# A hybrid attention encoder layer on one core: three placements in the schedule and the output norm's inverse root on GpSimd

## The chip, the cores and the metric

The kernel runs on one core of a Trainium2 chip. The metric is the device time of one execution in microseconds (us). The core has TensorE (PE, matrix products; its weight loads are listed as PEld), VectorE (DVE), ScalarE (ACT), GpSimd (POOL) and SyncE (SP, which issues nearly all the transfers here). Each engine executes its own instructions strictly in order and waits on semaphores for the others. A tile in PSUM, the memory that matrix products are written to, can be written again only when its last reader is done.

## The reference

Input x is 2048 x 1024, float32. One projection gives the columns of two mixers: gated linear attention (GLA: four heads, forward and backward scans, summed) and latent attention (MLA: four heads, low-rank query and key/value, softmax over all 2048 positions). Their gated outputs, 512 columns each, go through one output projection, and a layer norm over the scaled residual gives the result:

```python
def reference(x, ...):
    mixed = hybrid_mixer(x, ...)
    return layer_norm(DEEPNORM_ALPHA * x + mixed, ln_g, ln_b)

def hybrid_mixer(x, positions, w_in, ...):
    h = x @ w_in
    ... = jnp.split(h, idx, axis=-1)
    o_a = gla_branch(...)      # o = rms_norm(o_fwd + o_bwd, norm_g); return o * silu(gate)
    o_b = mla_branch(...)      # s = q_nope k_nope + q_rope k_rope; softmax(s) v; return o * silu(gate)
    return jnp.concatenate([o_a, o_b], axis=-1) @ w_out

def layer_norm(t, g, b):
    mu = jnp.mean(t32, axis=-1, keepdims=True)
    var = jnp.mean(jnp.square(t32 - mu), axis=-1, keepdims=True)
    return (t32 - mu) * lax.rsqrt(var + LN_EPS) * g + b
```

## The kernel before

The 2048 positions are cut into 16 chunks of 128. Every float32 product that needs the accuracy is made of three fast passes: each operand is split into a high part (`hi`, L378, on ACT, by rounding) and a low part (`lo`, L384, on DVE or POOL), and `mm3` (L432 to L434) adds high x high, low x high and high x low in PSUM.

The program has four stages. Sweeps A and B (to about 347 us) make the projections and scans of the linear attention. **Sweep C** (about 347 to 572 us) walks over the chunks two at a time, in 8 steps (st). For each chunk it projects the latent inputs (`ipm`, L1363), normalises and transposes them (`cq`, `ckv`, `tm`), finishes the linear attention's output, and for each step makes the gate of the second mixer. The pieces that matter here are these.

- The GLA output of a chunk: `Ob` is a matrix product in PSUM; `oib` (L1531, DVE) adds the part inside the chunk; `sqO` (L1535, ACT) squares; `ss` (L1540, L1541, DVE) sums; `rgl` and `rgd` make the inverse root; `og` (L1551, DVE) multiplies and so reads `Ob` for the last time; `oT` (L1557) transposes.
- The gate of a step: `pz` is a PSUM tile with a half for each of the two chunks, j = 0 and 1; `gm1`, `gm2`, `gm3` (L1287, L1291, L1295, ACT) make its sigmoid; `gm4` (L1299, DVE) multiplies; `gmx` (L1303, DVE) transposes into `gm`, which SP stores (L1309, `gm_s`).
- The queries of a step: `pqr` and its rope, and `pq`, a PSUM tile. `Ob`, `pz` and `pq` share one PSUM pool (`gp`), so that a new tile of one waits for the last reader of an older one of another.

The order of the instructions in sweep C is given by tables of due places, in units of a step: a task stands where its number says, for instance `gm1=(0.855, 1.309)` for the chunks j = 0 and 1 of a step. `PLACE_C` holds for the middle steps, `PLACE_C_FIRST` for the first step, `PLACE_C_LAST` for the last. The places move an instruction in the queue of its own engine; no data dependence changes.

**Attention** (about 572 to 1100 us) is a loop over 16 blocks i of 512 queries of one head, with 8 tiles j of 256 keys each. `scores` (L1633 to L1637) writes ten matmuls into a PSUM tile of two halves e, of which there are two in all; `copy` (L1642, ACT) takes it out; `smax` (L1652, L1655, DVE) keeps a running maximum in `rm`. At the end of a block `tmax` (L1661, PE) transposes `rm`, `rmax` (L1666, DVE) reduces it to `mc`, and `bmax` (L1673, PE) spreads it to the PSUM tile `mb`. Then `sub` (L1679, DVE), `exp` (L1683, ACT) and the product with the values follow, interleaved with the scores of the next block. Here too a list of places sets the order: `put(t, ...)` puts a call at place t = 8 i + j.

The **output projection** (about 1100 to 1252 us) works chunk by chunk on 16 chunks: the gate (`of`, L1999) and the low parts (`ol`) on POOL, `oh` on ACT, 48 matmuls, then on DVE the residual (L2066; L2057 for the last chunk), the statistics `bn`, their mean and variance `mv` (L2075), `u` = variance + epsilon (L2076), two passes that subtract the mean and scale (L2078), the inverse root of u, and two passes that multiply by it and add the shift (L2081). Each of these two is followed by a store (L2082, SP). The inverse root is `rsqrt`: a logarithm and an exponential on ACT (L445, L446), and a Newton step as three instructions on DVE (L452 to L454).

Of the kernel before, what the change touches and what calls it, by code (L numbers as in the profile page):

```python
# [9 lines left out]
F32 = mybir.dt.float32  # L10
# [3 lines left out]
ALU = mybir.AluOpType  # L14
# [4 lines left out]
P = 128  # L19
# [10 lines left out]
QB = 512  # L30
# [107 lines left out]
    tq=(1.44, 1.56),  # L138
# [4 lines left out]
    kvx=(1.06, 1.48),  # L143
# [15 lines left out]
    kvx=(1.3, 1.44),  # L159
# [7 lines left out]
    tq=(1.13, 1.56),  # L167
    xh=(-0.19, -0.054),
    sqO=(0.272, 0.94),
    rgl=(0.283, 1.029),  # L170
# [10 lines left out]
    oT=(0.392, 1.103),  # L181
    oib=(0.24, 0.881),
    ss=(0.278, 1.005),
    rgd=(0.359, 1.067),
    og=(0.391, 1.102),
    ssm=(0.277, 0.958),
    rmd=(0.401, 1.006),
# [20 lines left out]
    gm1=(0.45, 0.823),  # L208
    gm2=(0.46, 0.826),
    gm3=(0.47, 0.829),  # L210
    gm4=(0.745, 0.832),
    gmx=(0.76, 0.835),
# [20 lines left out]
)  # L233
PLACE_C_FIRST = dict(
    skv=1.6,
    kvx=(1.18, 1.5),
    ipa=(-1.874, 0.381),
    ipb=(-1.582, 0.655),
    ipc=(-0.643, 0.818),
# [1 line left out]
    Ob=(0.066, 0.896),  # L241
    tm=(0.445, 1.143),
    pqr=(0.716, 1.336),
    tq=(1.18, 1.53),
    xh=(-0.3, 1.403),
    sqO=(0.469, 0.999),
    rgl=(0.603, 1.027),
    sqm=(0.073, 0.865),
    rml=(0.101, 0.976),
    cq=(0.33, 1.098),  # L250
# [4 lines left out]
    ckvTh=(0.483, 1.183),  # L255
    krT=(0.871, 1.252),
    qrTh=(1.276, 1.598),
    oT=(0.805, 1.172),
    oib=(0.459, 0.956),
    ss=(0.596, 1.015),  # L260
    rgd=(0.636, 1.064),
    og=(0.804, 1.171),
    ssm=(0.095, 0.913),
    rmd=(0.194, 1.009),
    krf=(-0.407, 0.869),
    cqTl=(0.579, 1.316),
    ckvTl=(0.54, 1.33),
# [17 lines left out]
    gm1=(0.623, 0.643),  # L285
    gm2=(0.6231, 0.815),
    gm3=(0.6232, 0.82),
    gm4=(0.65, 0.83),
    gmx=(0.81, 0.835),
    sgm=1.056,  # L290
    pq=1.431,
    qah=1.57,
# [12 lines left out]
    tq=(0.95, 2.1),  # L305
    xh=(-0.262, -0.109),
    sqO=(0.15, 0.4265),
    rgl=(0.229, 0.429),
# [10 lines left out]
    oT=(0.4285, 0.432),  # L319
    oib=(0.063, 0.426),  # L320
    ss=(0.188, 0.428),
    rgd=(0.25, 0.43),
    og=(0.26, 0.431),
    ssm=(0.1025, 0.53),
    rmd=(0.427, 0.605),
# [17 lines left out]
    lx=(-0.48, -0.573),  # L343
    soT=(1.29, 2.304),
    pz=(0.572, 0.578, 0.707, 0.845, 0.918, 1.023, 1.1, 1.22),
    gm1=(0.855, 1.309),
    gm2=(0.91, 1.608),
    gm3=(1.2, 1.859),
    gm4=(1.26, 1.953),
    gmx=(1.265, 1.954),  # L350
    sgm=2.042,
    pq=1.525,
    qah=1.948,
# [13 lines left out]
class K:  # L367
    def __init__(self, tc, ins, out):
        self.tc, self.nc, self.ins, self.out = tc, tc.nc, ins, out
        self.ulate = []  # L370
        self.qt = {}
        self.parts = {}
# [1236 lines left out]
    def attention(self):  # L1609
        tc, nc = self.tc, self.nc  # L1610
        mm = nc.tensor.matmul
        V, G, Ac = nc.vector, nc.gpsimd, nc.scalar
        NP = NKT // 2
        with ExitStack() as ctx:
# [5 lines left out]
            pM, pO, pX, pA, pS = bank("pM"), bank("pO"), bank("pX"), bank("pA"), bank("pS", 2)  # L1620
# [1 line left out]
            nb = len(blocks)  # L1622
            stt = [dict(s=[None] * NP) for _ in blocks]

            def scores(i, j):


                d = stt[i]
                qh, ql, rh, rl = self.qt[i]
                ps = d["ps", j] = pS.tile([P, 2, QB], F32, tag="pS", name=f"pS{i}_{j}")  # L1630
                for e in range(2):
                    kh, kl, kr = (t[:, 2 * j + e] for t in (self.ckvT_h, self.ckvT_l, self.kr))
                    mm(ps[:, e], kh, qh, start=True, stop=False)  # L1633
                    mm(ps[:, e], kh, ql, start=False, stop=False)  # L1634
                    mm(ps[:, e], kl, qh, start=False, stop=False)  # L1635
                    mm(ps[:, e], kr, rh, start=False, stop=False)  # L1636
                    mm(ps[:, e], kr, rl, start=False, stop=True)  # L1637
# [183 lines left out]
            def put(place, fn, *a):  # L1821
                todo.append((place, len(todo), fn, a))

            def at(f, i, j=None):
                p = PLACE_LAST.get(f, PLACE[f]) if i == nb - 1 else PLACE[f]
                return p[j] if isinstance(p, tuple) else p
# [6 lines left out]
            for i in range(nb):  # L1833
                for j in range(NP):
                    t = NP * i + j
                    put(t, scores, i, j)
                    for n, f in (("copy", copy), ("max", smax), ("sub", sub), ("exp", exp), ("hi", phi), ("lo", plo),
                                 ("pv", pv), ("acc", acc)):
                        if n != "acc" or j != SUM_POOL[0] or i == nb - 1:
                            put(t + at(n, i, j), f, i, j)  # L1840
                put(NP * i + at("acc0", i), acc0, i)
                for n, f in (("tmax", tmax), ("rmax", rmax), ("bmax", bmax)) + {nb - 1: (), nb - 2: own_late}.get(i, own):
                    put(NP * i + NP - 1 + at(n, i), f, i)
                if i + 2 < nb:
                    put(NP * i + 4.05, self.fetch, i + 2)
# [93 lines left out]
class OutProj:  # L1939
# [3 lines left out]
    def __init__(self, kern, ctx, qp, bp, sp, ps, pa, pb, pc, pd):  # L1943
        self.k, self.nc, self.qp, self.bp, self.sp, self.ps = kern, kern.nc, qp, bp, sp, ps
        self.single = (pa, "mb"), (pb, "x"), (pc, "o"), (pd, "ap")
        self.sm = ctx.enter_context(kern.tc.tile_pool(name="smo", bufs=2, reuse_waits="tile"))
        self.raw, self.W, self.gr = {}, {}, {}

    def slot(self, name, dt=F32):
# [119 lines left out]
    def finish(self, o):  # L2069
        kern, nc, sm = self.k, self.nc, self.sm  # L2070
        V, Ac = nc.vector, nc.scalar
        c, rr = o["c"], o["rr"]
        mv = sm.tile([P, 2], F32, tag="mv", name=f"mv{c}")
        u = sm.tile([P, 1], F32, tag="u", name=f"u{c}")
        V.bn_aggr(mv, o["bn"])  # L2075
        V.tensor_scalar(u, mv[:, 1:2], LN_EPS, None, ALU.add)  # L2076
        for n in range(2):
            V.scalar_tensor_tensor(rr[:, n], rr[:, n], mv[:, 0:1], self.ln[0][:, n], ALU.subtract, ALU.mult)  # L2078
        rs = kern.rsqrt(sm, u, 1, f"ln{c}")
        for n in range(2):  # L2080
            V.scalar_tensor_tensor(rr[:, n], rr[:, n], rs, self.ln[1][:, n], ALU.mult, ALU.add)  # L2081
            nc.sync.dma_start(kern.out[c * P:(c + 1) * P, n * 512:(n + 1) * 512], rr[:, n])  # L2082
# [70 lines left out]
```

## Time and profile before

| what | us |
|---|---|
| median of three runs | 1254.19 (1253.59 to 1255.71) |
| the profiled execution | 1253.2 |
| its span, first to last instruction | 1251.4 |
| TensorE busy | 1231.4 |
| VectorE busy | 910.5 |
| ScalarE busy | 732.5 |
| GpSimd busy | 727.8 |

The granted TensorE clock was 0.998 of full speed. In a timeline a row gives the start, the duration, the engine, the line, the operation with its output and inputs, the shapes, and in brackets how long the engine had stood idle before it and what ended the wait. Buffer numbers are left out of the names, and neighbouring instructions of one kind are drawn together (x2, x3). In a list of waits the three numbers are the total, the times and the longest.

### The profile page before, as it was taken

To read this page: it belongs to the slowest core of one execution; us is meant where nothing else is said; L and a number is where in the kernel's file an instruction comes from. 1 tells how busy PE (TensorE), PEld (TensorE's weight loads), DVE (VectorE), ACT (ScalarE), POOL (GpSimd) and SP (SyncE) were. 2 spreads that over 40 slices of the span, in tenths; PEclk is the share of its full clock that TensorE was granted. 3 is DMA by queue.
4 is the path that set the end of the run, shared out by engine and by line. 5 is a ranking of instruction groups with operands and counts; after the bars stand their busy time and mean duration, and the time that the engine had idled before them with its cause. 6 is when DMAs were issued, how large, how long until landed. Compare 5 with 4: busy or idle time off the path is not lost.

```text
span 1251.4 us, 18903 instructions
## 1 busy us (share of the span) xinstructions
PE 1231.4 (98%) x6464; PEld 1066.7 (85%) x6464; DVE 910.5 (73%) x1698; ACT 732.5 (59%) x1173; POOL 727.8 (58%) x443
## 2 busy tenths in 40 slices
PE   8999999999999999999999999999999999999997
PEld 7999999999888889888788888888888888888886
DVE  6635454544566777675999999999999998388776
ACT  7543434344565555545888888888888888411110
POOL 0132323232345555521798888889999999954650
PEclk9999999999999999999999999999999999999999
DMA  8224555555757888859543333313356310376652
GB/s 297 76 80 128 136 143 139 142 136 147 260 178 210 247 253 245 256 177 209 92 69 65 60 59 62 75 24 76 76 112 123 79 43 25 126 241 220 202 189 82
DMA packets 311568, 173.95 MB, mean 139 GB/s; under 512 B 212806, under 2 KB 264910, under 8 KB 311472
## 3 DMA queue, kind: packets, MB, share of 16 engines
q1 hardware_dynamic: 310352, 170.62, 51.0%
q0 software_dynamic: 672, 2.10, 0.4%
q8 instruction: 51, 0.84, 0.3%
q14 instruction: 45, 0.37, 0.1%
q10 hardware_dynamic: 448, 0.03, 0.0%
HBM read 113.93 MB, written 67.14 MB: 145 GB/s over the span
## 4 chain that ended last, share of the span: by engine, by line
PE 90%; DVE 3%; ACT 2%; issue 2%; DMA 2%; POOL 1%; SPq 0%; DVEq 0%; POOLq 0%; ACTq 0%
PE ipm L1363 5%; PE o L432 5%; PE o L434 5%; PE o L433 5%; PE pS L1633 5%; PE pS L1635 5%; PE pS L1634 5%; PE pS L1637 5%; PE pS L1636 5%; PE ipa L432 4%; PE ipa L434 4%; PE ipa L433 4%; PE po L433 3%; PE po L434 3%; PE po L432 3%; PE ipg L434 2%
## 5 line engine op out<-in xcount | busy, mean ns | idle before, releaser
L384 POOL TENSOR_TENSOR pl<-s,ph 128x1024 fp32r<-128x1024 f32 x128 | 306.7, 2414 | 47.2 <-ACT ph L378 37.0
L1642 ACT ACTIVATE s<-pS 128x1024 f32<-128x1024 f32 x128 | 131.4, 1027 | 52.1 <-PE pS L1637 47.1
L1655 DVE TENSOR_TENSOR rm<-pS,rm 128x512 f32<-128x512 f32 x210 | 144.8, 689 | 18.2 <-ACT s L1642 12.7
L1679 DVE TENSOR_TENSOR s<-s,mb 128x1024 f32<-128x1024 f32 x128 | 151.2, 1213 | 8.9 <-PE mb L1673 8.8
L378 ACT ACTIVATE ph<-s 128x1024 fp32r<-128x1024 f32 x128 | 134.8, 1056 | 15.6 <-PE o L434 15.0
L1683 ACT ACTIVATE s<-s 128x1024 f32<-128x1024 f32 x128 | 131.5, 1051 | 10.5 <-DVE s L1679 9.6
L432 PE MATMUL ipa<-wah,xah 128*128 128x384 f32 (+1 forms) x384 | 128.5, 335 | 5.0 <-ACT wah L378 5.0
L433 PE MATMUL ipa<-wal,xah 128*128 128x384 f32 (+1 forms) x384 | 124.3, 324 | 0.6 <-DVE wal L384 0.5
L434 PE MATMUL ipa<-wah,xal 128*128 128x384 f32 (+1 forms) x384 | 124.1, 323 | 0.0
L1105 POOL TENSOR_TENSOR Sb<-Sb,Us 64x512 f32<-64x512 f32 x15 | 19.9, 1325 | 169.9 <-DVE Us L1097 160.8
L1633 PE MATMUL pS<-qh,kvT 128*128 128x512 f32 x256 | 102.6, 401 | 0.8 <-DVE rm L1655 0.4
L432 PE MATMUL o<-ph,vh 128*128 128x512 f32 x256 | 101.0, 395 | 0.0
L1635 PE MATMUL pS<-qh,kvT 128*128 128x512 f32 x256 | 100.0, 391 | 0.0
L1634 PE MATMUL pS<-ql,kvT 128*128 128x512 f32 x256 | 99.9, 390 | 0.0
L1637 PE MATMUL pS<-rl,kvT 128*128 128x512 f32 x256 | 99.8, 390 | 0.0
L1636 PE MATMUL pS<-rh,kvT 128*128 128x512 f32 x256 | 99.7, 390 | 0.0
L434 PE MATMUL o<-ph,vl 128*128 128x512 f32 x256 | 99.7, 390 | 0.0
L433 PE MATMUL o<-pl,vh 128*128 128x512 f32 x256 | 99.6, 389 | 0.0
L1706 DVE TENSOR_TENSOR ap<-ap,s 128x512 f32<-128x512 f32 x120 | 82.9, 691 | 2.6 <-ACT s L1683 0.7
L432 PEld LDWEIGHTS ipa<-wah,xah 128*128 128x128 f32 x384 | 72.6, 189 | 8.4 <-ACT wah L378 5.6
L433 PEld LDWEIGHTS ipa<-wal,xah 128*128 128x128 f32 x384 | 72.7, 189 | 1.9 <-DVE wal L384 1.4
L384 POOL TENSOR_TENSOR ol<-of,oh 128x512 fp32r<-128x512 f32 x32 | 42.6, 1332 | 52.5 <-ACT oh L378 47.1
(309 smaller groups left out, 3286.3 us busy)
## 6 DMA issues: line engine op xcount, KB each, us to landing
xcf<-xT_dram SPq DMA_DIRECT2D x16, 512.0 KB, 5.4
xr<-x_dram SPq DMA_DIRECT2D x16, 512.0 KB, 6.4
out_dram<-rr SPq DMA_DIRECT2D x32, 256.0 KB, 3.8
xaf<-xT_dram SPq DMA_DIRECT2D x14, 512.0 KB, 4.2
oib<-oi_s SPq DMA_DIRECT2D x16, 256.0 KB, 4.8
qdb<-qd_s SPq DMA_DIRECT2D x16, 256.0 KB, 3.5
SU<-su_s SPq DMA_DIRECT2D x16, 256.0 KB, 5.0
ub<-u_s SPq DMA_DIRECT2D x16, 256.0 KB, 4.2
```

The source lines that it names most:

```text
L378: return nc.scalar.activation(dst, src, AF.Copy).ins
L384: return e.tensor_tensor(dst, src, hi.bitcast(F32), ALU.subtract).ins
L432: mm(out, ah, bh, start=start, stop=False)
L433: mm(out, ah, bl, start=False, stop=False)
L434: mm(out, al, bh, start=False, stop=stop)
L1633: mm(ps[:, e], kh, qh, start=True, stop=False)
L1634: mm(ps[:, e], kh, ql, start=False, stop=False)
L1635: mm(ps[:, e], kl, qh, start=False, stop=False)
L1636: mm(ps[:, e], kr, rh, start=False, stop=False)
L1637: mm(ps[:, e], kr, rl, start=False, stop=True)
L1655: V.tensor_tensor(d["rm"], src[:, e], d["rm"], ALU.max)
L1679: V.tensor_tensor(s, s, d["mb"][:, None, :].to_broadcast([P, 2, QB]), ALU.subtract)
```

## The change

Four things change.

1. In `PLACE_C_FIRST`, the first step of sweep C, the last part of chunk 1's linear-attention output moves ahead of the second gate's transposes and of the key/value transposes (`kvx`, `tq`).
2. In `PLACE_C_LAST`, the last step, the sigmoid of the first gate (`gm1` to `gmx`, j = 0) moves from 0.855 behind 1.25, past work of the next chunk.
3. In attention the scores of the second block's second tile are put as two halves, the first 0.6 of a place earlier, so that it stands ahead of `bmax` of the first block.
4. In the output norm the inverse root of u becomes one instruction on POOL, u to the power of −0.5, issued ahead of the two passes that subtract the mean. Logarithm, exponential and Newton step go away.

```diff
 PLACE_C_FIRST = dict(
-    kvx=(1.18, 1.5),
+    kvx=(1.245, 1.5),
...
-    tq=(1.18, 1.53),
+    tq=(1.246, 1.53),
...
-    sqO=(0.469, 0.999),
-    rgl=(0.603, 1.027),
+    sqO=(0.469, 0.941),
+    rgl=(0.603, 0.977),
...
-    oT=(0.805, 1.172),
-    oib=(0.459, 0.956),
-    ss=(0.596, 1.015),
-    rgd=(0.636, 1.064),
-    og=(0.804, 1.171),
+    oT=(0.805, 0.979),
+    oib=(0.459, 0.94),
+    ss=(0.596, 0.9455),
+    rgd=(0.636, 0.978),
+    og=(0.804, 0.9785),
...
-    rmd=(0.194, 1.009),
+    rmd=(0.194, 0.9775),
...
-    gm4=(0.65, 0.83),
-    gmx=(0.81, 0.835),
+    gm4=(0.65, 0.943),
+    gmx=(0.942, 0.9457),
...
 PLACE_C_LAST = dict(
-    gm1=(0.855, 1.309),
-    gm2=(0.91, 1.608),
-    gm3=(1.2, 1.859),
-    gm4=(1.26, 1.953),
-    gmx=(1.265, 1.954),
+    gm1=(1.25, 1.309),
+    gm2=(1.26, 1.608),
+    gm3=(1.27, 1.859),
+    gm4=(1.28, 1.953),
+    gmx=(1.285, 1.954),
...
-            def scores(i, j):
+            def scores(i, j, es=(0, 1)):
...
-                ps = d["ps", j] = pS.tile([P, 2, QB], F32, tag="pS", name=f"pS{i}_{j}")
-                for e in range(2):
+                if es[0] == 0:
+                    d["ps", j] = pS.tile([P, 2, QB], F32, tag="pS", name=f"pS{i}_{j}")
+                ps = d["ps", j]
+                for e in es:
...
-                    put(t, scores, i, j)
+                    if t == NP + 1:
+                        put(t - 0.6, scores, i, j, (0,))
+                        put(t, scores, i, j, (1,))
+                    else:
+                        put(t, scores, i, j)
...
+        self.half = self.sm.tile([P, 1], F32, tag="half", name="half", bufs=1)
+        kern.nc.gpsimd.memset(self.half, -0.5)
...
         V.tensor_scalar(u, mv[:, 1:2], LN_EPS, None, ALU.add)
+        rs = sm.tile([P, 1], F32, tag="rs", name=f"rs{c}")
+        nc.gpsimd.tensor_tensor(rs, u, self.half, ALU.pow)
         for n in range(2):
             V.scalar_tensor_tensor(rr[:, n], rr[:, n], mv[:, 0:1], self.ln[0][:, n], ALU.subtract, ALU.mult)
-        rs = kern.rsqrt(sm, u, 1, f"ln{c}")
```

In the changed kernel the lines of the output projection stand 8 to 9 further down (L1999 becomes L2007, L2078 becomes L2088, L2081 becomes L2090).

**VectorE in the first step of sweep C**, from the second transpose of the first step's gate (gm_4122, of pz_3985). Before (Ob_4184 is chunk 1's, qrf is the rope of a query, krf of a key):

```order
L1303 STREAM_TRANSPOSE gm_4122<-pz_3985 128x512
L1568 TENSOR_TENSOR krf_4179<-ipm_4056,cos 128x64
L1572 TENSOR_TENSOR rope_1_4180<-ipm_4056,sin 128x32 x2
L1376 TENSOR_SCALAR ssm_4176<-ssm_4176 128x1 x2
L1531 TENSOR_TENSOR Ob_4184<-Ob_4184,oib_3928 128x512
L1568 TENSOR_TENSOR qrf_4201<-pqr_4141,cos 128x256
L1572 TENSOR_TENSOR rope_0_4202<-pqr_4141,sin 128x4x32 x2
L456 TENSOR_TENSOR rm_t<-ipm_4056,ssm_4176 128x2
L457 TENSOR_TENSOR ipm_4056<-rm_t,ipm_4056 128x2
L458 TENSOR_SCALAR rm_t<-ipm_4056 128x2
L459 TENSOR_TENSOR rm_r<-rm_t,ipm_4056 128x2
L1540 TENSOR_REDUCE Ob_4184<-og_4221 128x4
```

And now, from the end of chunk 0's oT, with chunk 1's Ob as Ob_4181:

```order
L1568 TENSOR_TENSOR krf_4176<-ipm_4056,cos 128x64
L1572 TENSOR_TENSOR rope_1_4177<-ipm_4056,sin 128x32 x2
L1376 TENSOR_SCALAR ssm_4173<-ssm_4173 128x1 x2
L1531 TENSOR_TENSOR Ob_4181<-Ob_4181,oib_3928 128x512
L1303 STREAM_TRANSPOSE gm_4122<-pz_3985 128x512
L1299 TENSOR_TENSOR pz_3985<-pz_3985,gm_4122 128x512
L1540 TENSOR_REDUCE Ob_4181<-og_4197 128x4
L1541 TENSOR_SCALAR ss_4201<-Ob_4181 128x4
L1303 STREAM_TRANSPOSE gm_4122<-pz_3985 128x512
L1568 TENSOR_TENSOR qrf_4206<-pqr_4141,cos 128x256
L1572 TENSOR_TENSOR rope_0_4207<-pqr_4141,sin 128x4x32 x2
```

The key's rope and the addition of oib now stand ahead of both gate transposes (the last of them is the first row of the order before), and the reduction of chunk 1 stands between them, where before it stood behind the query's rope and the inverse root of the latent norm.

**ScalarE in the last step of sweep C**, from chunk 14's key split (krs) on. Before, with gm_6626 and pz_6574 the gate of this step:

```order
L1287 ACTIVATE gm_6626<-pz_6574 128x512
L378 ACTIVATE vh<-ckv_6493 128x128
L1291 ACTIVATE gm_6626<-gm_6626 128x512
L378 ACTIVATE qrT_6661<-qrx_6652 128x256
L1390 ACTIVATE ckv_6663<-ipm_6398,rm_r 128x128
L378 ACTIVATE kvT<-tm_6666 128x128
L378 ACTIVATE cqT_h_6558<-tm_6666 128x2x128
L1295 ACTIVATE gm_6626<-gm_6626 128x512
L378 ACTIVATE vh<-ckv_6663 128x128
```

And now, with the gate as gm_6697:

```order
L378 ACTIVATE vh<-ckv_6493 128x128
L378 ACTIVATE qrT_6658<-qrx_6649 128x256
L1390 ACTIVATE ckv_6660<-ipm_6398,rm_r 128x128
L378 ACTIVATE kvT<-tm_6663 128x128
L378 ACTIVATE cqT_h_6558<-tm_6663 128x2x128
L1287 ACTIVATE gm_6697<-pz_6574 128x512
L378 ACTIVATE vh<-ckv_6660 128x128
L1291 ACTIVATE gm_6697<-gm_6697 128x512
L1295 ACTIVATE gm_6697<-gm_6697 128x512
```

The three passes of the first gate now follow one another behind cqT_h of the last chunk; before, the first of them stood ahead of its latent split vh, and the third behind cqT_h.

**GpSimd in the output projection**, the last chunks. Before, the low parts (ol) and the gate (of) of chunks 14 and 15:

```order
L384 TENSOR_TENSOR ol_0_12594<-of_12419,oh_0_12592 128x512
L1999 TENSOR_TENSOR of_12419<-of_12419,gr_11694 128x512 x2
L384 TENSOR_TENSOR ol_1_12600<-of_12419,oh_1_12598 128x512
L384 TENSOR_TENSOR ol_0_12681<-of_12511,oh_0_12679 128x512
L1999 TENSOR_TENSOR of_12511<-of_12511,gr_11704 128x512 x2
L384 TENSOR_TENSOR ol_1_12687<-of_12511,oh_1_12685 128x512
```

And now, with rs_12582 the power of chunk 12 and of_12436 the gate of chunk 15:

```order
L2086 TENSOR_TENSOR rs_12582<-u_12579,half 128x1
L384 TENSOR_TENSOR ol_0_12592<-of_12436,oh_0_12590 128x512
L2007 TENSOR_TENSOR of_12436<-of_12436,gr_11706 128x512 x2
L384 TENSOR_TENSOR ol_1_12598<-of_12436,oh_1_12596 128x512
L2086 TENSOR_TENSOR rs_12661<-u_12658,half 128x1
L2086 TENSOR_TENSOR rs_12731<-u_12728,half 128x1
L2086 TENSOR_TENSOR rs_12826<-u_12823,half 128x1
```

Each power stands behind the low parts of the chunk two further on and ahead of those of the one after; the last three follow one another at the end.

## Prediction

> **What bounds the kernel now.** I read the page's first table, then the list of TensorE's waits, then the timelines around each wait.
>
> ```profile
> span 1251.4 us, 18903 instructions
> PE 1231.4 (98%) x6464; PEld 1066.7 (85%) x6464; DVE 910.5 (73%) x1698; ACT 732.5 (59%) x1173; POOL 727.8 (58%) x443
> PE pz L432 <- ACT gm L1287: 1.8, 1, 1.8
> PE pz L432 <- DVE og L1551: 1.1, 1, 1.1
> PE mb L1673 <- DVE mc L1666: 0.8, 1, 0.8
> PE pq L432 <- DVE og L1551: 0.6, 2, 0.4
> ```
>
> TensorE (PE) is busy for 98% of the span, so only its idle moments and the tail behind its last matmul can be saved. In the wait rows (total, times, longest) the four places of the change stand: sweep C's last step (1.8), its first step (1.1, and 0.4 of the 0.6), and one broadcast in attention (0.8). The list has no row for the output projection: PE never waits for the norm there, so the new norm can pay only at the end. The profiled run took 1253.2 us, 1.8 around the span, against a median of 1254.19; I work out differences on this trace and put them on the median.
>
> **A. Sweep C, first step.**
>
> ```profile
> 371.59 0.71 DVE L1557 STREAM_TRANSPOSE oT<-og 128x512 f32<-128x512 f32 x1
> 372.49 0.19 ACT L1371 ACTIVATION_READ_ACCUMULATOR sqm<-ipm 128x1 f32 x1
> 373.74 0.72 DVE L1303 STREAM_TRANSPOSE gm<-pz 128x512 f32<-128x512 f32 x1
> 376.77 0.69 DVE L1540 TENSOR_REDUCE Ob<-og 128x4 f32<-128x512 f32 x1
> 378.13 0.16 DVE L456 TENSOR_TENSOR rg_t<-Ob,ss 128x4 f32<-128x4 f32 x1 [0.48 <-ACT Ob L446]
> 378.92 1.13 DVE L1551 SCALAR_TENSOR_TENSOR og<-Ob,rg_r,ub 128x128 f32<-128x128 f32 x4
> 380.10 0.50 PE L432 MATMUL pz<-wzh,xch 128*128 128x512 f32 x1 [1.11 <-DVE og L1551]
> 381.92 0.69 DVE L1531 TENSOR_TENSOR Ob<-Ob,oib 128x512 f32<-128x512 f32 x1
> 383.28 0.69 DVE L1540 TENSOR_REDUCE Ob<-og 128x4 f32<-128x512 f32 x1 [0.56 <-ACT og L1535]
> 385.79 1.13 DVE L1551 SCALAR_TENSOR_TENSOR og<-Ob,rg_r,ub 128x128 f32<-128x128 f32 x4
> 387.06 0.36 PE L432 MATMUL pq<-cqT_h,wabs_h 128*128 128x256 f32 x1 [0.39 <-DVE og L1551]
> ```
>
> DVE (VectorE) executes the same instructions ahead of chunk 2's first og as before; only their order changes. So the move saves no work there, only idle time: the reduction of 376.77 comes some 1.6 us earlier, and the 0.48 us that DVE waited for ACT at 378.13 falls away. In exchange krf now stands first and must wait for ACT's read of ipm, done at 372.49 + 0.19 = 372.68, while DVE is free at 371.59 + 0.71 = 372.30: about 0.3 back. Net 0.18, so pz starts near 379.92, not 1.11 earlier. The second half is better: krf, rope and oib of the next chunk pass the three kvx and the qrx transposes, oib comes from 381.92 to about 380.84, and the 0.56 wait of 383.28 goes with it. By the durations above og ends near 386.1 instead of 386.92. PE's work between 380.10 and 387.06 is 6.96 − 0.39 = 6.57, so it reaches pq at 379.92 + 6.57 = 386.49 and finds og done. A is 0.18 + 0.39 = **−0.57 us**; the bounds are both waits whole, −1.5, and nothing. SP's store of gm waits for the second gm transpose, which moves from 373.74 to about 375.9:
>
> ```profile
> 374.48 0.37 SPq L1309 DMA_DIRECT2D gm_s<-gm  x1
> 374.91 1.44 SPq L1489 DMA_DIRECT2D ub<-u_s  x1
> 385.12 0.37 SPq L1340 DMA_DIRECT2D qr_s<-qrT  x1
> ```
>
> The loads queued behind it (ub, SU, oib) are issued about 1.9 us later. The next og, at 385, is the first to read that ub, and SP's queue is idle up to 385.12, so I cost this at nothing; without that cover it would cost the 1.9 less the room of og.
>
> **B. Sweep C, last step.**
>
> ```profile
> 562.47 0.50 PE L432 MATMUL pz<-wzh,xch 128*128 128x512 f32 x1 [1.82 <-ACT gm L1287]
> 564.29 0.35 ACT L1390 ACTIVATE ckv<-ipm,rm_r 128x128 f32<-128x128 f32 x1
> 565.68 0.48 PE L432 MATMUL pz<-wzh,xch 128*128 128x512 f32 x1
> 568.78 0.70 DVE L1299 TENSOR_TENSOR pz<-pz,gm 128x512 f32<-128x512 f32 x1 [1.81 <-PE pz L434]
> 570.32 0.60 ACT L1287 ACTIVATE gm<-pz 128x512 f32<-128x512 f32 x1 [3.10 <-DVE gm L1303]
> 571.64 0.64 ACT L1295 ACTIVATE gm<-gm 128x512 f32<-128x512 f32 x1
> 574.51 1.03 ACT L1642 ACTIVATE s<-pS 128x1024 f32<-128x1024 f32 x1
> 576.58 0.39 PE L1633 MATMUL pS<-qh,kvT 128*128 128x512 f32 x1
> ```
>
> The first gate exponential no longer stands between pz's halves, so the second half starts at 560.65 and the 1.82 is gone. But PE's next transposes need ckv, and ACT (ScalarE) still makes it at 564.29 + 0.35 = 564.64 behind work that is not moved; pz's last part comes at about 564.81 instead of 565.68: 0.87 stays, 0.95 turns into a wait for ckv. Now the price: gm1 must wait for all of pz, whose last matmul now ends 0.87 before the 568.7 that the product of 568.78 waited for, near 567.85, and gm1, gm2, gm3 (0.60 to 0.64 each) run only then, so the product starts near 569.86 and the second gm1 near 571.37, 1.05 after its 570.32. Everything behind it on ACT shifts by that, the copy of the first scores too: from 574.51 to 575.56, ending at 576.59. The third scores tile reuses that PSUM buffer. It started at 576.58, would like 575.71, and gets about 576.62. B is **0.0 us**: the stall goes from pz to the third scores tile. Bounds: −0.87 if ACT's chain is shorter than I make it, +1.05 if PE gains nothing while ACT's chain is later.
>
> **C. One scores tile split.**
>
> ```profile
> 594.35 0.65 PE L1673 MATMUL mb<-ident,mc 128*128 128x128 f32 x4 [0.78 <-DVE mc L1666]
> 595.04 3.48 DVE L1679 TENSOR_TENSOR s<-s,mb 128x1024 f32<-128x1024 f32 x3
> 598.44 1.41 DVE L1655 TENSOR_TENSOR rm<-pS,rm 128x512 f32<-128x512 f32 x2
> 599.99 0.47 PE L1633 MATMUL pS<-qh,kvT 128*128 128x512 f32 x1 [0.42 <-DVE rm L1655]
> ```
>
> Five matmuls (about 1.24 us) fill the 0.78 ahead of mb, so mb starts at about 594.56, 0.21 late. Three subtractions and two maxima follow on DVE with no gap, and the scores tile at 599.99 already waited 0.42 for that chain. It comes 0.21 later whatever PE did in between: C is **+0.2 us**, with −0.78 (the whole wait) and +0.4 as bounds.
>
> **D. The power.**
>
> ```profile
> 1244.80 0.15 DVE L2076 TENSOR_SCALAR u<-mv 128x1 f32<-128x1 f32 x1
> 1244.87 1.40 DVE L2078 SCALAR_TENSOR_TENSOR rr<-rr,mv,lng 128x512 f32<-128x512 f32 x2
> 1246.93 1.42 DVE L2081 SCALAR_TENSOR_TENSOR rr<-rr,ln_r,lnb 128x512 f32<-128x512 f32 x2
> L2148 POOL MEMSET const-float32-0.0<- 128x1 f32 x1 | 0.1, 103 | 0.2 <-issue 0.2
> L384 POOL TENSOR_TENSOR krs<-krf,krs 128x64 fp32r<-128x64 f32 x16 | 5.1, 318 | 10.7 <-ACT krs L378 10.7
> L384 POOL TENSOR_TENSOR ol<-of,oh 128x512 fp32r<-128x512 f32 x32 | 42.6, 1332 | 52.5 <-ACT oh L378 47.1
> ```
>
> Logarithm and exponential already hid under the two passes of 1244.87; what leaves the tail is the three Newton steps, 1246.93 − 1246.27 = 0.66 us. The power of length d runs on POOL (GpSimd) from u's end at 1244.95, beside those passes. But DVE and POOL slow each other:
>
> ```profile
> 1155.09 2.75 DVE L2081 SCALAR_TENSOR_TENSOR rr<-rr,ln_r,lnb 128x512 f32<-128x512 f32 x2
> 1155.54 3.45 POOL L1999 TENSOR_TENSOR of<-of,gr 128x512 f32<-128x512 f32 x2
> ```
>
> Beside POOL's gate the two passes took 2.75 instead of 1.42, as if the engines took turns (0.70, 1.32, 0.70, 1.32 gives just these ends), so I charge d in full: the gain is 0.66 − d. [...] No row shows a power. Its bounds are the 128x1 memset, 0.10, and a 128x512 pass, 1.33; by its size it is nearest to the memset and the 0.318 us of 128x64, and I take 0.25 for it. D is **−0.4 us** (−0.56 to +0.67). Earlier chunks: POOL's queue now holds each power behind a later chunk's gate and ahead of the next ol, where it waits for u as ACT's logarithm did. POOL idled 52.5 us before its ol, and the next oh no longer queues behind the logarithm on ACT; with no PE wait there, 15 powers, one memset and the removed 2 ACT and 3 DVE instructions per chunk cost and save nothing.
>
> **Sum**: −0.57 + 0.0 + 0.2 − 0.4 = −0.8 us, so 1254.19 − 0.8 = 1253.4. About 0.2% (2.5 us) is what a measurement of this kernel can tell from no change.
>
> **The rivals.**
> 1. *The stalls vanish instead of moving.* A gives its 1.5, B 0.87, C 0.78, D 0.56: −3.7, so 1250.5. For it: all are real idle time of PE. Against: in each of the three places a row shows the next wait ready behind (ckv, the score copy, rm).
> 2. *The power is slow* (slower). POOL's tail then sets the end: the time is −0.4 (A to C) + d − 0.66 from before; slower from about d = 1, and by over 0.2% from d = 3.5. At twice the 128x512 pass, 2.66 us, it is +1.6: 1255.8. From about d = 3.3, POOL's 52.5 us of idle time spread over 16 chunks, POOL would also set the pace of the projection, and the time would be 1256.5 or more. For it: no power in the trace, and a power is no add. Against: one element per partition. [...]
> 3. *The moves don't reach PE*: A's first wait comes back through krf and B loses ACT's 1.05. A 0, B +1.0, C +0.2, D −0.4: +0.8, 1255.0.
>
> **How the numbers follow.** Forecast 0.45 (own range 1252.3 to 1254.6), rival 1 0.26, rival 2 0.17, rival 3 0.12. Faster by over 0.2% (below 1251.7): rival 1 nearly whole, 0.25 with a little of the forecast. Slower by over 0.2% (above 1256.7): the long powers of rival 2 and the upper end of rival 3, 0.17. Within: 0.58. The range 1250.4 to 1256.4 takes in the bounds of the parts and rival 2 up to d = 3.
>
> **What would show it.** Right: PE's waits for gm and mb gone, pz's wait near 0.9, new PE waits of about 0.9 at the third scores tile and 0.9 for ckv in sweep C; 0.6 at the fourth tile of the second block; a power of 0.2 to 0.4 us; L2081's successor starting about 0.4 earlier after PE's last matmul. Wrong: a power above 1 us, PE waits in the output projection, or no new wait in attention while the span falls by 3 us.

## The result and the profile after

| | before | changed |
|---|---|---|
| median, us | 1254.51 (12 runs) | 1257.41 (12 runs) |
| ratio to before | | 1.0024 (95% interval 1.0016 to 1.0032) |
| span of the profiled execution | 1251.4 | 1254.8 |

The change costs about 3 us. The list of TensorE's waits in the changed kernel (total, times, longest) shows the first half of the reason. Its largest row, the wait at the start of the program, is left out here: it is 5.0 us before and 5.3 now.

```profile
span 1254.8 us, 18838 instructions
...
PE px L432 <- DVE rr L2074: 2.4, 1, 2.4
PE pS L1635 <- DVE rm L1657: 1.5, 1, 1.5
PE tm L1435 <- ACT ckv L1390: 1.1, 1, 1.1
PE pz L432 <- DVE og L1551: 0.9, 1, 0.9
PE pS L1635 <- ACT s L1644: 0.6, 1, 0.6
```

The lower four are the waits of the prediction, at their places. The first is new: in the output projection, where the kernel before has no wait at all, the product of chunk 4 waits for a residual of chunk 2. Its PSUM tile px is the one that chunk 2's second half lay in, and VectorE (DVE) reads that late. VectorE's timeline there, in the kernel before (ln_r ends a Newton step, L2081 are the two final passes of a norm, L2066 is the residual that reads PSUM):

```profile
1108.08 0.69 DVE L2066 SCALAR_TENSOR_TENSOR rr<-xr,pmb 128x512 f32<-128x512 f32 x1 [1.54 <-POOL of L1999]
1111.59 0.20 DVE L454 TENSOR_SCALAR ln_r<-ln_t,ln_y 128x1 f32<-128x1 f32 x1
1111.76 0.68 DVE L2066 SCALAR_TENSOR_TENSOR rr<-xr,px 128x512 f32<-128x512 f32 x1
1112.36 3.34 DVE L2081 SCALAR_TENSOR_TENSOR rr<-rr,ln_r,lnb 128x512 f32<-128x512 f32 x2
...
1116.50 0.39 PE L432 MATMUL px<-woh,oh 128*128 128x512 f32 x1
```

(the last row is TensorE's first matmul into px for chunk 4), and in the changed one:

```profile
1107.99 0.69 DVE L2074 SCALAR_TENSOR_TENSOR rr<-xr,pmb 128x512 f32<-128x512 f32 x1 [1.77 <-POOL of L2007]
1111.86 5.82 DVE L2090 SCALAR_TENSOR_TENSOR rr<-rr,rs,lnb 128x512 f32<-128x512 f32 x4 [3.18 <-POOL rs L2086]
1117.60 0.68 DVE L2075 BATCH_NORM_STATS2 bn<-rr 128x6 f32<-128x512 f32 x1
1118.21 0.67 DVE L2074 SCALAR_TENSOR_TENSOR rr<-xr,px 128x512 f32<-128x512 f32 x1
...
1118.92 0.50 PE L432 MATMUL px<-woh,oh 128*128 128x512 f32 x1 [2.42 <-DVE rr L2074]
```

Before, the residual of px stands ahead of all four final passes of chunks 0 and 1. Now it stands behind them, and they take 5.82 us. Two such passes take 1.41 us in the tail, where GpSimd (POOL) is idle; here GpSimd works nearly all the while, on a power, its low parts and its gate, and the prediction's row of two passes at 2.75 us beside the gate fits that. The residual ends at 1118.88 instead of 1112.44, and chunk 4's product, which reached px at 1116.50 before, waits.

The code leaves this order free. `LATE_ORDER` holds ScalarE, GpSimd and SyncE to the written order in this stage; VectorE's queue is left to the scheduler. Why it chose so is not shown; the two orders suggest that with the Newton step the final passes hung on a chain of small instructions, so that the residual came in between, and that with the power all four were placed at once.

The second half of the loss stands in no list of waits. Windows of 2 us of the changed kernel (us, busy time of each engine, granted clock of TensorE, DMA):

```profile
1114.00:1116.00 2.00, 2.00 (x11) 1.65 (x10) 2.00 (x3) 0.00 (x0) 1.92 (x2) 1.00 0.61 190
1116.00:1118.00 2.00, 0.50 (x3) 0.08 (x1) 2.00 (x2) 0.83 (x2) 1.26 (x2) 1.00 0.68 184
1118.00:1120.00 2.00, 1.07 (x5) 0.88 (x6) 1.90 (x6) 0.31 (x1) 1.14 (x1) 1.00 1.01 400
1120.00:1122.00 2.00, 2.00 (x6) 1.58 (x5) 2.00 (x4) 0.00 (x0) 1.89 (x2) 0.50 1.02 386
1122.00:1124.00 2.00, 2.00 (x7) 1.55 (x6) 2.00 (x2) 0.00 (x0) 2.00 (x2) 0.65 0.89 261
```

At 1120.01, 1.1 us after TensorE starts again, its clock falls to half. TensorE counts as busy there, but does 6 and 7 matmuls in 2 us instead of 10 or 11. The half product of 24 matmuls takes 7.23 us (1118.92 to 1126.15) where it took 5.44: 1.8 us more. So a wait of 2.4 us costs 4.2 here.

The tail, on the other hand, is shorter:

```profile
1248.97 0.15 DVE L2084 TENSOR_SCALAR u<-mv 128x1 f32<-128x1 f32 x1
1249.05 1.40 DVE L2088 SCALAR_TENSOR_TENSOR rr<-rr,mv,lng 128x512 f32<-128x512 f32 x2
1249.27 0.92 POOL L2086 TENSOR_TENSOR rs<-u,half 128x1 f32<-128x1 f32 x1 [9.76 <-DVE u L2084]
1250.37 1.41 DVE L2090 SCALAR_TENSOR_TENSOR rr<-rr,rs,lnb 128x512 f32<-128x512 f32 x2
```

From u to the final passes it takes 1250.37 − 1248.97 = 1.40 us; before it took 1246.93 − 1244.80 = 2.13. The power of 0.92 is hidden whole.

To add up the two profiled executions, I take at certain TensorE instructions the difference of their starts, changed minus before:

| stretch | change, us |
|---|---|
| sweeps A and B, untouched | +0.3 |
| A, first step of sweep C and what follows | −0.8 |
| B, last step and the first scores | +0.1 |
| C, the first maximum and the split tile | +0.1 |
| the rest of attention | +0.2 |
| the wait for px | +2.6 |
| the slow product behind it | +1.8 |
| the tail | −0.7 |
| sum | +3.6; the spans differ by 3.4 |

### The profile page after: what moved, and what is told of

It reads as the page before. It is cut to its first block, busy times and chain, and to the rows that moved or that the text cites. A ratio compares the mean times of both kernels' runs of the same rounds, so it can differ in the third digit from the quotient of the medians.

```text
span 1254.8 us, 18838 instructions
## 1 busy us (share of the span) xinstructions
PE 1233.8 (98%) x6464; PEld 1068.3 (85%) x6464; DVE 907.2 (72%) x1650; ACT 726.1 (58%) x1141; POOL 743.6 (59%) x460
## 4 chain that ended last, share of the span: by engine, by line
PE 89%; DVE 4%; ACT 2%; issue 2%; DMA 2%; POOL 1%; SPq 0%; DVEq 0%; POOLq 0%; ACTq 0%
PE ipm L1363 5%; PE o L432 5%; PE o L433 5%; PE o L434 5%; PE pS L1635 5%; PE pS L1637 4%; PE pS L1636 4%; PE pS L1639 4%; PE pS L1638 4%; PE ipa L432 4%; PE ipa L434 4%; PE ipa L433 4%; PE po L434 2%; PE po L432 2%; PE po L433 2%; PE ipg L434 2%
## 5 line engine op out<-in xcount | busy, mean ns | idle before, releaser
L378 ACT ACTIVATE oh<-of 128x512 fp32r<-128x512 f32 x32 | 19.2, 625 | 122.6 <-POOL of L2007 114.6
```

What stands on the lines that cost most here:

```text
L378: return nc.scalar.activation(dst, src, AF.Copy).ins
```

## The experiments

### Parts A, B and C alone; part D alone

```diff
 A, B, C as in the change
-        rs = sm.tile([P, 1], F32, tag="rs", name=f"rs{c}")
-        nc.gpsimd.tensor_tensor(rs, u, self.half, ALU.pow)
+        rs = kern.rsqrt(sm, u, 1, f"ln{c}")
```

> Parts A, B and C alone, with the old norm. Theory (the whole loss is made in the output projection, by the order of VectorE's queue around chunk 2's second residual): no wait of TensorE for px, span about 1250.8, 0.6 below before (A -0.8, B and C +0.2 together), time about 0.5 us below before. Rival (the moves in sweep C and attention cost): 1 us or more above before.

Measured: 1252.96 against 1253.79 for before (0.9991, interval 0.9982 to 1.0001), span 1251.2, no wait for px. By the starts of TensorE's instructions A is −0.7, B +0.2, C +0.1.

The other half of the change, with the tables and the scores of before:

> Part D alone, sweep C and attention as before. Theory: the px wait of 2.4 us stands again, with 1.8 us of slow matmuls behind it, less 0.7 at the tail: span about 1254.9, time 3.5 us above before. Rival (the loss comes from A to C): within 1 us of before.

Measured: 1255.97 (1.0019, 1.0010 to 1.0028), span 1255.3, with a px wait of 2.6 us. In the trace the px product is 2.9 us late at its start and 4.7 at its end, as expected; the median is 2.2 above before, less than the 3.5 expected. The profiled execution, which has the slow product, has a mean clock of 0.997. Of the ten, five have a mean clock of 0.999 and take 1255.47 on average, the three at 0.997 take 1257.05, and two more, at 0.998 and 0.995, take 1257.63 and 1259.08: by these clocks the slow product does not come in every execution. (The kernel before has executions at 0.997 as well, without a px wait; they come up under B below.) The loss is in D, and the rival (A to C) has fallen.

### Chunk 2's residual first

```diff
+                op.residual(rest[2], 0)
+                op.residual(rest[2], 1)
                 for c in (0, 1):
                     op.finish(rest[c])
...
-                    op.residual(rest[c], 0)
-                    op.residual(rest[c], 1)
+                    if c == 3:
+                        op.residual(rest[c], 0)
+                        op.residual(rest[c], 1)
```

> The changed kernel with both residuals of chunk 2 written ahead of the norms of chunks 0 and 1, so that VectorE reads px before the four final passes; power, POOL's queue and SP's queue unchanged. Theory: px wait and slow matmuls gone, 4.2 us back: span about 1250.6, time about 0.8 us below before. Rival (the power itself costs, by its length or by its place in POOL's queue): time stays 2 us or more above before.

Measured: 1252.70 (0.9989, 0.9980 to 0.9999), span 1249.9. VectorE and TensorE there:

```profile
1107.13 0.69 DVE L2077 SCALAR_TENSOR_TENSOR rr<-xr,pmb 128x512 f32<-128x512 f32 x1 [1.33 <-POOL of L2010]
1107.74 0.68 DVE L2077 SCALAR_TENSOR_TENSOR rr<-xr,px 128x512 f32<-128x512 f32 x1
...
1111.04 5.84 DVE L2093 SCALAR_TENSOR_TENSOR rr<-rr,rs,lnb 128x512 f32<-128x512 f32 x4 [1.43 <-POOL rs L2089]
...
1115.80 0.39 PE L432 MATMUL px<-woh,oh 128*128 128x512 f32 x1
```

The four passes still come together and still take 5.84 us, the power still waits in GpSimd's queue, and nothing is lost: px is read at 1107.74. So neither the power's length, nor its place on GpSimd, nor the slowed passes cost anything that shows here; their place ahead of one residual did. The span of this one execution flatters the order: TensorE is already 0.96 us ahead of before at 31.76 us, in a stretch that no part of the change touches. The medians are the better measure. Run again beside the changed kernel on one chip:

> The changed kernel once more, on the chip of the next run, to compare the two directly: 3 us above before; px wait of 2.4 us and a slow product behind it.

> resid_first once more with more rounds: 1 us below before (ratio 0.9990), 4 us below the changed kernel on the same chip; no px wait.

The changed kernel took 1257.30 (1.0021, 1.0012 to 1.0031) with a px wait of 3.1 us; the reordered one 1253.17 (0.9989, 0.9980 to 0.9998), 4.1 less. It beats the changed kernel clearly, and before by about 0.1%, with intervals that end just short of no change (0.9999 and 0.9998).

### The old norm with the late residual

```diff
-                    op.residual(rest[c], 1)
+                    with self.after(*[rest[n]["end"].ins for n in (0, 1) if c == 2]):
+                        op.residual(rest[c], 1)
```

Here `end` is the last final pass of a chunk; the rest is the kernel before, with logarithm, exponential and Newton step.

> The kernel before, with logarithm, exponential and Newton step, but chunk 2's second residual held back behind the final passes of chunks 0 and 1 on VectorE, as the changed kernel has it. Theory (the order alone does it): a px wait of about 2.5 us and slow matmuls behind it, span about 1255.5, time 4 us above before, with no power in the program. Rival (the power does it): as before, within 1 us.

Measured: 1256.12 (1.0013, 1.0004 to 1.0022), span 1254.4:

```profile
1113.13 3.20 DVE L2082 SCALAR_TENSOR_TENSOR rr<-rr,ln_r,lnb 128x512 f32<-128x512 f32 x2
1116.49 2.19 DVE L2082 SCALAR_TENSOR_TENSOR rr<-rr,ln_r,lnb 128x512 f32<-128x512 f32 x2
1118.60 0.68 DVE L2067 SCALAR_TENSOR_TENSOR rr<-xr,px 128x512 f32<-128x512 f32 x1
...
1119.34 0.50 PE L432 MATMUL px<-woh,oh 128*128 128x512 f32 x1 [2.31 <-DVE rr L2067]
1119.67 0.39 PE L433 MATMUL px<-wol,oh 128*128 128x512 f32 x1
```

The order makes the wait without any power in the program. The slow product did not follow in this execution: the half product took 5.58 us (1119.34 to 1124.92) at a clock of 1.00. The expectation was wrong in that, and so was the time, 2.3 above before and not 4.

### What makes the product slow

To keep TensorE busy while it waits for px, 11 matmuls into an unused tile stand ahead of the second half of chunk 4's product:

```diff
         for n in range(2):
+            if o["c"] == 4 and n == 1:
+                t = self.single[3][0].tile([P, 512], F32, tag=self.single[3][1], name="busy")
+                for k in range(11):
+                    self.k.nc.tensor.matmul(t, o["oh"][0][:, 0], self.W[0][0][:, :512], start=True, stop=True)
             for k in range(NK):
```

> The changed kernel with 11 extra matmuls (128x512, about 2.5 us) into an unused PSUM tile ahead of the second half of chunk 4's product, where TensorE waits for px; their result is not used, the output stays the reference's. Theory (the second part of the loss is the clock, which drops after the idle stretch): the px product still starts at about 1118.9, but its 24 matmuls take 5.4 us and not 7.2, the granted clock stays at 1.00, and the span is about 1.8 below the changed kernel's, 1253.0. Rival (the slow matmuls come from contention with the other engines' traffic at that moment, not from idleness): they stay slow, span 1254.8.

```profile
1116.83 2.65 PE L2045 MATMUL busy<-woh,oh 128*128 128x512 f32 x11
1119.34 0.50 PE L432 MATMUL px<-woh,oh 128*128 128x512 f32 x1
...
1124.93 0.39 PE L432 MATMUL po<-woh,oh 128*128 128x512 f32 x1
```

px starts as late as in the changed kernel (2.5 us late, taken from the instructions ahead of it), and its product takes 5.59 us. The time is 1255.72 (1.0012, 1.0004 to 1.0021), 1.8 above before where the changed kernel is 2.9 and 3.2 above it in its two measurements; the span is 1253.7. So the drop followed TensorE's idleness here and not the traffic of the other engines, whose program is the same: with the gap filled all ten executions have a mean clock of 0.998 or 0.999, and 2.65 us of extra work in the gap take 1.6 us off the product behind it.

With 2 matmuls in place of 11 I asked whether the length of the idle stretch decides:

> As busy_in_wait, but with 2 extra matmuls in place of 11, so that TensorE stands idle about 2.0 us and not 2.4. The clock stayed at 1.00 after an idle 2.31 us in old_norm_late_resid and dropped after 2.42 and 2.62. If the length of the idle stretch decides, it stays at 1.00 here and the px product takes 5.5 us; if the share of busy time over a longer window decides, it drops as in the changed kernel and the product takes 6.5 to 7.2.

```profile
1115.95 0.61 PE L2045 MATMUL busy<-woh,oh 128*128 128x512 f32 x2
1118.47 0.50 PE L432 MATMUL px<-woh,oh 128*128 128x512 f32 x1 [1.91 <-DVE rr L2078]
...
1119.51 0.48 PE L433 MATMUL px<-wol,oh 128*128 128x512 f32 x1
1119.78 0.63 PE L434 MATMUL px<-woh,ol 128*128 128x512 f32 x1
...
1122.77 0.55 PE L432 MATMUL px<-woh,oh 128*128 128x512 f32 x1
```

The clock dropped after 1.91 us idle (it is 0.50 from 1120 to 1122), though it had stayed up after 2.31 us in the old norm's run. So the length of the stretch alone did not decide; that theory has fallen. The granted clock in the kept traces shows in what the cases differ.

In the four traces with a drop amid the work the half clock lasts 3.413 us, here from 1119.68 to 1123.09. The next drop stands in the tail, behind the last matmul, and comes 126.29 or 129.71 us after the first one's end, which is 37 or 38 times 3.413. So in these traces the clock changed on a grid of steps of 3.41 us, which lay elsewhere in the program in each of them. Here is the step that holds most of each idle stretch; in the old norm's trace, which has no drop amid the work, its place is an estimate, counted back from the drop in the tail, at 1248.44, by 38 such steps:

| trace | idle stretch, us | the step | idle within it, us | clock behind it |
|---|---|---|---|---|
| changed | 2.42 | 1116.59 to 1120.01 | 2.33 | half |
| d_only | 2.62 | 1117.15 to 1120.56 | 2.28 | half |
| two_busy | 1.91 | 1116.26 to 1119.68 | 1.91 | half |
| changed_again | 3.05 | 1117.05 to 1120.46 | 2.61 | half |
| old_norm_late_resid | 2.31 | 1115.32 to 1118.73 | 1.70 | full |

By that count the old norm's 2.31 us were cut in two by a step's edge, 1.70 and 0.61. Amid the work behind the start of the program, in all twelve traces, the steps with 1.91 us idle or more, the four of the table, are followed by half the clock, and no step with 1.70 or less is. So the idle time within one step sorts the cases seen here, where the length of the stretch does not. No run moved the grid on purpose: that the clock went by the steps is my estimate from the agreement of these traces.

### The price of a power

```diff
+        r0 = sm.tile([P, 1], F32, tag="r0", name=f"r0{c}")
+        nc.gpsimd.tensor_tensor(r0, u, self.half, ALU.pow)
         nc.gpsimd.tensor_tensor(rs, u, self.half, ALU.pow)
```

> resid_first with two powers in a row per chunk on GpSimd, the first into a tile that nobody reads. At the tail: if a power is 0.92 us of work by itself, the final passes start 0.75 later than in resid_first (the second power ends 1.84 after 1244.36). If, as the pair of 1.09 us in the changed kernel's trace suggests, a power alone takes about 0.5 and the rest is a wait for VectorE's pass, they start about 0.4 later. No wait for px in either case.

GpSimd with an idle VectorE (first two rows), and both engines at the tail:

```profile
1112.15 0.56 POOL L2090 TENSOR_TENSOR r<-u,half 128x1 f32<-128x1 f32 x1
1112.69 0.54 POOL L2091 TENSOR_TENSOR rs<-u,half 128x1 f32<-128x1 f32 x1
...
1246.80 1.40 DVE L2093 SCALAR_TENSOR_TENSOR rr<-rr,mv,lng 128x512 f32<-128x512 f32 x2
1247.02 0.92 POOL L2090 TENSOR_TENSOR r<-u,half 128x1 f32<-128x1 f32 x1 [9.10 <-DVE u L2087]
1247.92 0.69 POOL L2091 TENSOR_TENSOR rs<-u,half 128x1 f32<-128x1 f32 x1
1248.64 1.42 DVE L2095 SCALAR_TENSOR_TENSOR rr<-rr,rs,lnb 128x512 f32<-128x512 f32 x2 [0.44 <-POOL rs L2091]
```

A power with VectorE idle takes 0.54 us. Beside VectorE's two passes the first takes 0.92, and VectorE pays nothing: its two passes take 1.40, as with GpSimd idle. The final passes start 0.44 late, as the second theory had it. The same 0.44 stood in most chunks, and TensorE waited 1.3 us more in one place (span 1253.1, one time of 1255.23): VectorE stood 2.21 us for the second power in chunk 4, where resid_first has no wait, and 0.45 and 0.44 in the next two, and behind these passes stood a reduction that TensorE needed. Here the wait on VectorE was paid by what was queued behind it.

### A and D with the residual first, without B and C

> Parts A and D with both residuals of chunk 2 first, without B and C, which the traces put at about +0.2 together. Theory: span about 1249.7, time 1.2 to 1.5 us below before and level with or up to 0.3 below resid_first. Rival (B and C gain after all): above resid_first by 0.3 or more.

Measured: 1253.73 (0.9993, 0.9984 to 1.0001), span 1251.2. The forecast of 1.2 to 1.5 below before was missed: it is 0.2 below, where resid_first is 1.1 and 1.0 below. That is the rival's side, but the intervals overlap, and A itself was not steady between these runs (below), so whether B and C cost 0.2 or gain stays open by the times alone. What speaks for a gain stands under B below.

## Why the prediction was wrong

The forecast was 1253.4 (1250.4 to 1256.4), the measured time 1257.41.

**The step that failed** is the one on the earlier chunks: "with no PE wait there, 15 powers, one memset and the removed 2 ACT and 3 DVE instructions per chunk cost and save nothing". It followed the power through GpSimd's queue, where it was right, and did not look at VectorE's, which the scheduler reorders. Absence of a wait in the trace of before said that the slack was enough for the order of before. px was read 4.06 us ahead of its need there (1112.44 against 1116.50); the new order took 6.4 from it. The prediction had itself named TensorE waits in the output projection as a sign of being wrong. The experiments bear it out from both sides: the order without the power makes the wait, the power without the order doesn't.

**The price of a wait** was taken to be its length. Here it was 2.4 us of idleness and 1.8 of half clock behind it. No rival had that. The half clock lasted 3.41 us, and 1.91 to 2.61 us idle within one step stood ahead of it.

**A** was forecast at −0.57 and measured −0.78 in the changed kernel and −0.7 in abc_only. The mechanism was right: pz still waits (0.88), and pq no longer does. One of its terms was misread: krf's wait is 372.68 − 372.30 = 0.38 by the prediction's own rows and not 0.3, which would have made the first part 0.10 and A −0.49.

```profile
380.35 0.50 PE L432 MATMUL pz<-wzh,xch 128*128 128x512 f32 x1 [0.88 <-DVE og L1551]
386.65 0.28 PE L432 MATMUL pq<-cqT_h,wabs_h 128*128 128x256 f32 x1
```

It is not steady, though. In resid_first and changed_again the pq wait came back (0.29 and 0.42), and A gave only 0.1 to 0.2 in this step. VectorE's split of qrT and a GpSimd multiplication (L1521) come at the same moment, and one of the two takes longer. In the changed kernel it is the multiplication, 1.31 us where it takes 1.03 in resid_first; there it is the split, by 0.7. Nine profiled executions have A's tables: in the four in which GpSimd starts first the split takes 1.12 to 1.26 us and pq waits 0.29 to 0.42, in the five others it takes 0.41 to 0.72 and pq does not wait. First the changed kernel:

```profile
384.01 0.41 DVE L384 TENSOR_TENSOR qrT<-qrx,qrT 128x256 fp32r<-128x256 f32 x1
...
384.01 1.31 POOL L1521 TENSOR_TENSOR SU<-Sf,cw 64x512 f32<-64x512 f32 x1
```

then resid_first:

```profile
382.78 1.12 DVE L384 TENSOR_TENSOR qrT<-qrx,qrT 128x256 fp32r<-128x256 f32 x1
...
382.59 1.03 POOL L1521 TENSOR_TENSOR SU<-Sf,cw 64x512 f32<-64x512 f32 x1
```

**B** was forecast at 0.0 and measured +0.1. The wait for gm is gone, 1.08 of it is a wait for ckv, and the third scores tile waits 0.65 where 0.9 was foreseen. That is read in executions in which the clock stayed up there; over many executions B may be worth more. The wait of 1.82 us that it takes away lies between the 1.70 and the 1.91 us idle in a step of the table above, so by my estimate the clock may drop behind it in some executions. Of the 75 executions of before that ran beside the experiments 28 have a mean clock of 0.997 or less and a median of 1255.2; the other 47 have 1253.6. In a_d_resid_first, which keeps this wait, 6 of 12 are at 0.997, and in abc_only, both runs of resid_first and busy_in_wait, which have B and C and no idle stretch at px, none of 41. The prediction did not see this. It is argued and not shown: no execution of before at the lower clock was profiled, and B was not run without C.

**C** was forecast at +0.2 and measured +0.1. mb came at its time plus 0.2, and the idle time moved to the fourth scores tile, 1.54 instead of 0.42:

```profile
564.16 0.33 PE L1435 MATMUL tm<-ident,ckv 128*128 128x128 f32 x1 [1.08 <-ACT ckv L1390]
576.05 0.50 PE L1635 MATMUL pS<-qh,kvT 128*128 128x512 f32 x1 [0.65 <-ACT s L1644]
599.77 0.47 PE L1635 MATMUL pS<-qh,kvT 128*128 128x512 f32 x1 [1.54 <-DVE rm L1657]
```

I had written that this tile would show 0.6; I had forgotten that TensorE arrives there earlier by the gain of the filled gap, so the whole 1.54 is to be seen, while the start, taken from the block's first maximum, is only 0.1 to 0.2 later.

**D's tail** was forecast at −0.4 and measured −0.7: two errors that went against each other. The power takes 0.92 there and not 0.25, and charging its length to VectorE was wrong: it fits under the two passes, and they are not slowed.

**The rivals.** Rival 1 (the stalls vanish) and rival 3 (the moves don't reach TensorE) were not what happened. Rival 2 had the right sign and the wrong mechanism: with a power of 0.92 us it forecasts no loss, and resid_first shows that this is so. The first two powers of the changed kernel took 1.09 us together.

## What to carry to other kernels

A change that makes a result ready earlier also lets a scheduler place its readers earlier; look at the queue of every engine whose order is not fixed, and at what stands behind the readers now. Writing the instructions that free a PSUM tile ahead of those that only finish an output guarded against this here and cost nothing that the runs show. And look at the clock behind a wait of TensorE: 2.42 us became 4.2 here, with half the clock behind them, and 2.31 us in old_norm_late_resid had no such price.

## What the runs showed of the hardware

- TensorE's granted clock fell to half with idle stretches of 1.91 (two_busy), 2.42 (changed), 2.62 (d_only) and 3.05 us (changed_again) amid dense work, and stayed up with 2.31 (old_norm_late_resid); with 11 matmuls in the gap (busy_in_wait) it stayed up. In these traces it changed on a grid of 3.41 us that lay elsewhere in each: steps with 1.91 us idle or more were followed by half the clock, steps with 1.70 or less were not.
- A 128x1 power on GpSimd took 0.54 us with VectorE idle (two_powers) and 0.92 to 1.0 beside VectorE's passes on two SBUF operands (changed), while those took their 1.40 unchanged: in the tail they ran from 1249.05 to 1250.45 and the power from 1249.27 to 1250.19. Beside 128x512 passes of GpSimd two such passes took 2.75 (before).
